# Full experts take silu times up with tokens on partitions and turn only the product; the expert sums move to other banks; the last normalisation runs without GpSimd

## The chip, the cores and the metric

One NeuronCore of a Trainium2 chip. The metric is the device time of one execution, in microseconds (us). TensorE (PE) multiplies and writes PSUM banks of 128 x 512 floats, VectorE (DVE), ScalarE (ACT) and GpSimd (POOL) work on 128 partitions, SyncE (SP) issues transfers. Each engine takes its own instructions in order; semaphores tie the engines together.

## The reference, cut to what matters

Two decoder layers of three mixed branches each; a dense feed-forward follows the first, a mixture of eight experts the second. The change lies in the experts and in the normalisation behind them:

```python
def swiglu(t, w_gu, w_down):
    gate, up = jnp.split(t @ w_gu, 2, axis=-1)
    return (jax.nn.silu(gate) * up) @ w_down

# x: 256 tokens x 1024; eight experts, each w_gu 1024 x 7168 and w_down 3584 x 1024, float32
top_val, top_idx = lax.top_k(logits, 2)
top_w = jax.nn.softmax(top_val, axis=-1)
combine = jnp.sum(jax.nn.one_hot(top_idx, 8) * top_w[..., None], axis=1)
for e in range(8):
    out = out + combine[:, e:e + 1] * swiglu(t, w_gu[e], w_down[e])
h = layer_norm(ALPHA * h + out, ln_ffn_g, ln_ffn_b)
```

## The kernel before, in words

**Precision.** A float32 number is split into a high part (`fp32r`) and the rest, the low part. A product of two float32 matrices is three products: high by high, high by low, low by high.

**Experts and their width.** `route` counts the tokens of each expert. An expert with more than 64 tokens is *full*: its 128 columns of `xe` are tokens, high and low parts being two matrices, and each 2048-column unit of weights takes 12 matmuls of 128 x 512. An expert with up to 64 tokens is a *half* one: `xe` holds the high and low part of each token side by side, so that a gate or up unit goes through PE as raw float32 with 64 columns and needs no split, and a down unit takes 8 matmuls. Which case an expert is in is known on the device only: `tc.If` on a register of each engine chooses. In this input experts 0, 3, 4 and 7 are full, 1, 2, 5 and 6 half (the lines of their matmuls in the trace tell: L1306 is the raw case).

**Steps, slots, units.** An expert has 7 steps (512 inner columns each). A step has six units of 1 MB: two of gate weights (slots 0, 1), two of the down weights of two steps ago (slots 2, 3), two of up weights (slots 4, 5). All steps of all experts form one list of 56, and the loop in `experts` writes out the order of every engine's work by hand (`manual_schedule`). SP loads units into a ring of 11 buffers (`load_unit`, as `make_low` frees them); ACT makes the high part (`make_high`, two units ahead, L1276), DVE the low part (`make_low`, one ahead, L1287); `products` issues the matmuls (L1306, L1311, L1313).

**What the change touches.** Per step `i`, before the change and for both kinds of expert alike:

- `evict(i, 0)` (L1342, slot 2) copies the gate sums from PSUM to `e0`, `evict(i, 1)` (next step's slot 0) the up sums to `e1`. Tokens lie on partitions there.
- `turn(i, half)` (L1348) turns both by four PE transposes each into a `tp` bank: half 0 in slot 4, half 1 in the next step's slot 2.
- `second` (L1352, ACT) and `total` (L1356, DVE) add the two columns of each token of a half expert; for a full expert `total` adds zero times the second, so that it only moves the turned sums back into `e0`, `e1`.
- `silu` (L1360) on the gate, `product` (L1363), then `inner` (L1374 on ACT, L1376 on DVE) writes the high and low part of the product into `f2`, which the down matmuls read.

`combine` (L1418) brings an expert's rows back to token order, two sums per half in `tp` banks, of which there are two; `add` (L1424) adds them to `oa`. `rows` (L1410, L1412) makes the high and low part that `combine` reads. `dispatch(e0)` (L1187 to L1223) gathers the tokens of the next two experts in the odd experts' steps; its last stage makes `sel` on DVE (L1218), turns it on PE (L1219) and copies it on DVE (L1222).

`finish_last` is the end: 8 matmuls (L1574), four `add`s, mean and variance by `bn_stats` on DVE, and one token block's scale and shift on GpSimd and DVE (L1608, L1609), the other's on DVE (L1603, L1605). Behind it every engine loads `cmax` and skips a second pass of the experts (for more than 128 tokens in one) that this input doesn't need.

Of the kernel before, what the change touches and what calls it, by code (L numbers as in the profile page):

```python
# [101 lines left out]
class Builder:  # L102
# [1079 lines left out]
    def dispatch(self, e0):  # L1182
# [27 lines left out]
        ps = self.ptp()  # L1210
        sel = self.tmp("sel", [P, 2, 2 * P], F32R, bufs=1)
        for k in range(2):
            e = slice(e0 + k, e0 + k + 1)

            at = self.tmp("at", [P, P], bufs=1)
            V.scalar_tensor_tensor(at, self.slot2, self.full[:, e], self.slot64, OP.mult, OP.add)
            for t in range(2):
                V.tensor_scalar(sel[:, t, k * P : (k + 1) * P], at, self.pos[:, t, e], None, OP.is_equal)  # L1218
                nc.tensor.matmul(ps[:, k * 256 + t * P : k * 256 + (t + 1) * P], sel[:, t, k * P : (k + 1) * P],  # L1219
                                 self.identr, start=True, stop=True)  # L1220
            st = self.tmp("st", [P, 2, P], F32R, bufs=3)
            V.tensor_copy(st.rearrange("p a b -> p (a b)"), ps[:, k * 256 : k * 256 + 256])  # L1222
            self.slots[e0 + k] = xe[k], st  # L1223
# [67 lines left out]
    def products(self, full, units):  # L1291
# [6 lines left out]
        def some(cases, unsplit):  # L1298
            for k, parts, first, last in units:
# [23 lines left out]
    def experts(self, base, first):  # L1323
# [16 lines left out]
        def evict(i, half):  # L1340
            g[i, half] = self.tmp(f"e{half}", [P, 512], bufs=2 - half)
            ACT(g[i, half], ps.pop((i, half)), AF.Copy)  # L1342

        def turn(i, half):
            tp = ps[i, half, "t"] = self.ptp()
            for q in range(4):
                s = slice(q * P, (q + 1) * P)
                nc.tensor.transpose(tp[:, s], g[i, half][:, s], self.ident)  # L1348

        def second(i, half):  # L1350

            ACT(split4(g[i, half])[:, :, 1, :], split4(ps[i, half, "t"])[:, :, 1, :], AF.Copy)  # L1352

        def total(i, half):
            gv, e = split4(g[i, half]), steps[i][0]
# [3 lines left out]
        def silu(i):  # L1359
            ACT(g[i, 0], g[i, 0], AF.Silu)  # L1360

        def product(i):
            V.tensor_mul(g[i, 1], g[i, 1], g.pop((i, 0)))  # L1363

        def inner(i, part):
# [6 lines left out]
            fv, u = f2[i].rearrange("p q a (n h) -> p a q h n", h=2), split4(g[i, 1])  # L1372
            if part == 0:
                ACT(fv[:, 0], u, AF.Copy)  # L1374
            else:
                V.tensor_sub(fv[:, 1], u, rr(fv[:, 0]))  # L1376
                del g[i, 1]

        def pair(k):
# [17 lines left out]
            self.products(fulls[e], units)  # L1397
# [16 lines left out]
        def combine(e, hf):  # L1414
            for t in range(2):
                sums[e, hf, t] = self.ptp()
# [4 lines left out]
        def add(e, hf):  # L1421
            s = slice(hf * 512, hf * 512 + 512)
            for t in range(2):
                V.scalar_tensor_tensor(self.oa[:, t, s], sums.pop((e, hf, t)), self.comb[:, t, e : e + 1],  # L1424
                                       self.oa[:, t, s], OP.mult, OP.add)

# [4 lines left out]
        with self.tc.manual_schedule():  # L1431
# [8 lines left out]
            for i, (e, j) in enumerate(steps):  # L1440
# [3 lines left out]
                if j == 2:  # L1444
                    value(e + 1)
                if e % 2 and j == 2 and e + 1 < N_EXPERTS:
                    nxt = self.dispatch(e + 1)
                for slot in range(6):
                    idle = slot in (2, 3) and i < 2

                    if slot == 2 and i:
                        turn(i - 1, 1)
                    if slot == 4:
                        turn(i, 0)
# [10 lines left out]
                    if slot == 0 and i:  # L1465
                        evict(i - 1, 1)
                        silu(i - 1)
                    if slot == 2:
                        evict(i, 0)
# [7 lines left out]
                    if slot == 5 and i:  # L1477
                        inner(i - 1, 1)
                    if after is not None and slot in (0, 2):
# [24 lines left out]
                    if slot % 2 == 0:  # L1504
                        pair(k)
# [6 lines left out]
            evict(last, 1)  # L1512
            silu(last)
            turn(last, 1)
            self.make_high(k + 2)
            second(last, 1)
            self.make_low(k + 1)
            total(last, 1)
            pair(k)
# [10 lines left out]
    def moe(self, l):  # L1530
# [13 lines left out]
        rv = nc.values_load(self.cmax[0:1, 0:1], min_val=0, max_val=SEQ)  # L1544
        with self.tc.If(rv > P):
# [6 lines left out]
    def finish_last(self, py, st, comb):  # L1552
# [9 lines left out]
        mv = self.tmp("fl_mv", [P, 2, 2])  # L1562
        rs = self.tmp("fl_rs", [P, 2])
        nm = self.tmp("fl_nm", [P, 1])
        st6 = self.tmp("fl_st", [P, 2, 2, 6], bufs=1)
# [16 lines left out]
        def stats(t, hf):  # L1582
            pin(V.bn_stats(st6[:, t, hf, :], self.oa[:, t, hf * 512 : hf * 512 + 512]))  # L1583

        def aggr(t):
            pin(V.bn_aggr(mv[:, t, :], st6[:, t].rearrange("p a b -> p (a b)")))
            pin(nc.scalar.activation(rs[:, t : t + 1], mv[:, t, 1:2], AF.Sqrt, bias=self.eps))

        x0, y0, x1, y1 = self.oa[:, 0, :], out[:, 0, :], self.oa[:, 1, :], out[:, 1, :]
        add(0, 0)  # L1590
        add(0, 1)
        stats(0, 0)
        stats(0, 1)
        add(1, 0)
        aggr(0)
        pin(V.reciprocal(rs[:, 0:1], rs[:, 0:1]))
        pin(V.scalar_tensor_tensor(nm, mv[:, 0, 0:1], -1.0, rs[:, 0:1], OP.mult, OP.mult))
# [116 lines left out]
```

## Time and profile before

| | us |
|---|---|
| three runs: median (lowest to highest) | 1815.33 (1814.37 to 1815.5) |
| the profiled execution | 1813.66 |
| its span, first to last instruction | 1811.9 |
| around the span | 1.76 |

Durations below are of the profiled execution, so sums are made against its 1813.66 us; the median of the runs lies 1.67 us (0.09%) above. The granted TensorE clock is 0.988 of full speed on the mean, 1.00 in the stretches that matter here. Over the span PE is busy 96%, DVE 72%, ACT 61%, POOL 16%. The experts take from about 890 us to the end.

### The profile page before, as it was taken

What the parts mean: (1) busy time and instruction counts of PE and PEld (TensorE: products, weight loads), DVE (VectorE), ACT (ScalarE), POOL (GpSimd) and SP (SyncE); (2) the same over time, 40 slices, a digit from 0 to 9 for tenths busy, and PEclk for the clock granted to TensorE, in tenths of its full rate; (3) what the DMA queues carried; (4) which work ended last, traced back from release to release, by engine and by line L of the source; (5) the groups of instructions that cost most, each with busy time, mean ns of one, the idle gap of its engine ahead of it and who ended that gap; (6) DMA issues with size and microseconds to landing.
All of it is one profiled execution on the core that took longest, in us unless ns stands there. A gap on an engine that the chain in (4) does not pass through costs nothing. (4 is left out here: it accounts for less than half of the span.)

```text
span 1811.9 us, 28892 instructions
## 1 busy us (share of the span) xinstructions
PE 1737.7 (96%) x10759; PEld 1433.1 (79%) x10759; DVE 1307.0 (72%) x1600; ACT 1097.0 (61%) x1539; POOL 291.0 (16%) x379
## 2 busy tenths in 40 slices
PE   8999999999999999999899999999999999988996
PEld 7989999899998999999788554457888855445784
DVE  7796675865568786665798555579899855557996
ACT  6565564554456665564587455467777745546873
POOL 6115731510033117640000000000000000000000
PEclk8999999999999999999999999999999999999998
DMA  5445545345455545557489999999888999999991
GB/s 211 158 132 185 167 160 173 134 163 184 132 176 173 169 146 194 173 197 273 161 332 361 402 418 418 418 418 418 351 349 345 355 396 419 418 418 419 419 388 47
DMA packets 74848, 497.20 MB, mean 274 GB/s; under 512 B 9340, under 2 KB 10924, under 8 KB 17324
## 3 DMA queue, kind: packets, MB, share of 16 engines
q1 hardware_dynamic: 69200, 486.64, 69.8%
q10 hardware_dynamic: 5468, 8.15, 1.6%
q8 instruction: 114, 1.87, 0.4%
q14 instruction: 66, 0.54, 0.1%
HBM read 493.65 MB, written 1.10 MB: 273 GB/s over the span
## 5 line engine op out<-in xcount | busy, mean ns | idle before, releaser
L1287 DVE TENSOR_TENSOR wlo<-raw,mhi 128x2048 fp32r<-128x2048 f32 x224 | 506.2, 2278 | 102.9 <-ACT mhi L1276 49.0
L1276 ACT ACTIVATE mhi<-raw 128x2048 fp32r<-128x2048 f32 x224 | 424.1, 1904 | 79.3 <-DMA raw<-in_down 47.7
L172 DVE TENSOR_TENSOR w<-raw,w 128x1024 fp32r<-128x1024 f32 (+2 forms) x260 | 320.3, 1232 | 163.4 <-ACT w L171 162.3
L198 PE MATMUL ps_mm<-HL,w 128*128 128x272 f32 (+2 forms) x1344 | 392.5, 292 | 0.8 <-DVE t L393 0.4
L199 PE MATMUL ps_mm<-HL,w 128*128 128x272 f32 (+2 forms) x1344 | 385.3, 287 | 1.1 <-DVE HL L377 1.1
L200 PE MATMUL ps_mm<-HL,w 128*128 128x272 f32 (+2 forms) x1344 | 385.9, 287 | 0.0
L171 ACT ACTIVATE w<-raw 128x1024 fp32r<-128x1024 f32 (+2 forms) x260 | 265.2, 1020 | 119.9 <-PE ps_mm L200 88.9
L198 PEld LDWEIGHTS ps_mm<-HL,w 128*128 128x128 f32 x1344 | 253.3, 188 | 3.9 <-issue 1.4
L199 PEld LDWEIGHTS ps_mm<-HL,w 128*128 128x128 f32 x1344 | 253.1, 188 | 1.7 <-DVE HL L377 1.3
L200 PEld LDWEIGHTS ps_mm<-HL,w 128*128 128x128 f32 x1344 | 253.0, 188 | 0.2 <-DVE w L172 0.2
L1311 PE MATMUL ps_mm<-mhi,xe 128*128 128x512 f32 x888 | 225.3, 395 | 0.1
L1306 PE MATMUL ps_mm<-raw,xf 128*64 128x512 f32 x896 | 201.1, 597 | 0.0
L1311 PEld LDWEIGHTS ps_mm<-mhi,xe 128*128 128x128 f32 x888 | 164.2, 188 | 37.7 <-ACT mhi L1276 1.6
L1311 PE MATMUL ps_acc<-mhi,f 128*128 128x512 f32 x672 | 179.7, 403 | 0.1
L1608 POOL TENSOR_TENSOR raw<-raw,gb 128x768 f32<-128x768 f32 x1 | 1.8, 1801 | 956.1 <-ACT raw L1598 956.1
L1306 PEld LDWEIGHTS ps_mm<-raw,xf 128*64 128x64 f32 x896 | 60.8, 137 | 112.5 <-issue 110.9
L1311 PEld LDWEIGHTS ps_acc<-mhi,f 128*128 128x128 f32 x672 | 124.6, 192 | 23.9 <-issue 0.2
L1313 PE MATMUL ps_acc<-wlo,f 128*128 128x512 f32 x448 | 124.7, 400 | 6.0 <-DVEq L1285 4.6
L1313 PE MATMUL ps_mm<-wlo,xe 128*128 128x512 f32 x444 | 121.3, 394 | 2.2 <-DVE wlo L1287 2.2
L1313 PEld LDWEIGHTS ps_acc<-wlo,f 128*128 128x128 f32 x448 | 85.4, 194 | 29.8 <-DVEq L1285 7.8
L492 POOL TENSOR_SCALAR seg<-b,ctm 128x16 f32<-128x16 f32 (+3 forms) x96 | 101.1, 1071 | 41.7 <-PE ps_acc L534 21.2
L1342 ACT ACTIVATE e<-ps_mm 128x512 f32<-128x512 f32 x112 | 66.8, 596 | 65.3 <-PE ps_mm L1313 50.3
(363 smaller groups left out, 2611.0 us busy)
## 6 DMA issues: line engine op xcount, KB each, us to landing
raw<-in_up SPq DMA_DIRECT2D x224, 1024.0 KB, 11.9
raw<-in_down SPq DMA_DIRECT2D x110, 1024.0 KB, 12.4
raw<-in_g SPq DMA_DIRECT2D x24, 1024.0 KB, 4.9
raw<-in_q SPq DMA_DIRECT2D x12, 1024.0 KB, 5.4
raw<-in_x SPq DMA_DIRECT2D x12, 1024.0 KB, 4.9
raw<-in_dg SPq DMA_DIRECT2D x11, 1024.0 KB, 5.0
raw<-in_du SPq DMA_DIRECT2D x11, 1024.0 KB, 4.8
raw<-in_dd SPq DMA_DIRECT2D x16, 704.0 KB, 4.1
```

What stands on the lines that cost most here:

```text
L171: pin(nc.scalar.activation(hv, src, AF.Copy))
L172: pin((eng or nc.vector).tensor_sub(lv, src, rr(hv)))
L198: nc.tensor.matmul(ps, h, a, start=first and k == 0, stop=False)
L199: nc.tensor.matmul(ps, h, b, start=False, stop=False)
L200: nc.tensor.matmul(ps, lo, a, start=False, stop=last and k == kn - 1)
L492: nc.gpsimd.tensor_scalar(seg[:, j, c0 : c0 + T - l0], ab[:, j, l0:T], self.ctm[:, ki, hd : hd + 1], 0.0, OP.subtract, OP.min)
L1276: d = self.nc.scalar.activation(hi[:, v], self.raws[k][:, v], AF.Copy)
L1287: self.nc.vector.tensor_sub(lo[:, v], self.raws[k][:, v], rr(self.whole[k][:, v]))
L1306: mm(ps[c : c + HALF], rows[:, q % 2 * 4 + i, :], self.raws[k][:, i * 512 : i * 512 + 512], start=bool(first) and i < 2, stop=bool(last) a ...
L1311: mm(ps, a, hv, start=i in first and c == 0, stop=False)
L1313: mm(ps, cases(x)[0], lv, start=False, stop=i in last)
L1342: ACT(g[i, half], ps.pop((i, half)), AF.Copy)
```

## The change

1. **Arms.** `arms` wraps an operation in `tc.If` on one engine with another body for full and half experts. For a full expert: `gate` writes silu of the gate sums straight from PSUM (ACT); `up` is nothing; `times` multiplies the up sums in PSUM by it on DVE (slot 1 of the next step); only half 1 is turned; `inner` reads the turned product from its `tp` bank. `second`, `total`, `product` and the turn of half 0 are skipped. Half experts keep the old order, with `total` a plain add and moved into `product` and `inner`.
2. **Where the turns are issued.** Most turns are issued inside the same If as the matmuls behind them (`before`); in the first two steps of an expert the turn of half 1 has an If of its own.
3. **Banks.** `combine`'s sums and the last stage of `dispatch` come from the four `mm` banks instead of the two `tp` banks. That stage of `dispatch` now makes all of `sel` first, turns it a slot later, and copies it on ACT.
4. **End.** `add` also writes row sums (`accum_out`), the squares are summed on ACT, scale and shift run on DVE alone; the output goes in four transfers of 256 KB, two on SP's queue, two on ACT's. `cmax` is loaded one step before the end.

```diff
@@ dispatch
-        ps = self.ptp()
...
+        if e0:
+            yield
+            yield
+        ps = self.pmm() if e0 else self.ptp()
+        for k in range(2):
+            for t in range(2):
                 nc.tensor.matmul(ps[:, k * 256 + t * P : k * 256 + (t + 1) * P], sel[:, t, k * P : (k + 1) * P],
                                  self.identr, start=True, stop=True)
+        if e0:
+            yield
+        for k in range(2):
             st = self.tmp("st", [P, 2, P], F32R, bufs=3)
-            V.tensor_copy(st.rearrange("p a b -> p (a b)"), ps[:, k * 256 : k * 256 + 256])
+            nc.scalar.activation(st.rearrange("p a b -> p (a b)"), ps[:, k * 256 : k * 256 + 256], AF.Copy)
@@ products.some
+            if before is not None:
+                before(cases is whole)
@@ experts
+        def arms(i, engine, full, half):
+            x = fulls[steps[i][0]]
+            if x is None:
+                if full is not None:
+                    full()
+            elif full is None:
+                with self.tc.If(x[engine] < 1):
+                    half()
+            else:
+                with self.tc.If(x[engine] > 0) as case:
+                    full()
+                if half is not None:
+                    with case.Else():
+                        half()
+        def gate(i):
+            g[i, 0] = self.tmp("e0", [P, 512], bufs=2)
+            x = ps.pop((i, 0))
+            arms(i, on.Activation, lambda: ACT(g[i, 0], x, AF.Silu), lambda: ACT(g[i, 0], x, AF.Copy))
+        def up(i):
+            g[i, 1] = self.tmp("e1", [P, 512], bufs=1)
+            def half():
+                ACT(g[i, 1], ps[i, 1], AF.Copy)
+                ACT(g[i, 0], g[i, 0], AF.Silu)
+            arms(i, on.Activation, None, half)
+        def times(i):
+            arms(i, on.DVE, lambda: V.tensor_mul(g[i, 1], ps[i, 1], g[i, 0]), None)
         def turn(i, half):
             tp = ps[i, half, "t"] = self.ptp()
-            for q in range(4):
+            def go(full):
+                if full and half == 0:
+                    return
+                for q in range(4):
...
         def total(i, half):
-            V.scalar_tensor_tensor(gv[:, :, 0, :], gv[:, :, 1, :], self.half[:, e : e + 1],
-                                   split4(ps.pop((i, half, "t")))[:, :, 0, :], OP.mult, OP.add)
+            V.tensor_add(gv[:, :, 0, :], gv[:, :, 1, :], split4(ps[i, half, "t"])[:, :, 0, :])
         def product(i):
-            V.tensor_mul(g[i, 1], g[i, 1], g.pop((i, 0)))
+            def go():
+                total(i, 1)
+                V.tensor_mul(g[i, 1], g[i, 1], g[i, 0])
+            arms(i, on.DVE, None, go)
@@ inner
+                arms(i, on.Activation, lambda: ACT(fv[:, 0], t, AF.Copy), lambda: ACT(fv[:, 0], u, AF.Copy))
...
+                low = lambda x: V.tensor_sub(fv[:, 1], x, rr(fv[:, 0]))
+                arms(i, on.DVE, lambda: low(t), half)
@@ combine
-                sums[e, hf, t] = self.ptp()
+                sums[e, hf, t] = self.pmm()
@@ the loop over steps and slots
+                    before = None
                     if slot == 2 and i:
-                        turn(i - 1, 1)
+                        before = turn(i - 1, 1)
+                        if j < 2:
+                            with_arms(i - 1, before)
+                            before = None
                     if slot == 4:
-                        turn(i, 0)
+                        before = turn(i, 0)
...
-                    if slot == 3 and i:
-                        total(i - 1, 1)
-                    if slot == 5:
-                        total(i, 0)
+                    if slot == 1 and i:
+                        times(i - 1)
@@ finish_last
-                                       OP.mult, OP.add))
+                                       OP.mult, OP.add, accum_out=part[:, t, hf : hf + 1]))
...
+        for t in range(2):
+            add(t, 0)
+            add(t, 1)
+            m, v = nm[:, t : t + 1], rs[:, t : t + 1]
+            pin(V.tensor_scalar(m, part[:, t, 0:1], part[:, t, 1:2], -1.0 / D_MODEL, OP.add, OP.mult))
+            pin(nc.scalar.activation(junk[t], self.oa[:, t, :], AF.Square, bias=m, accum_out=sq[:, t : t + 1]))
+            pin(nc.scalar.activation(v, sq[:, t : t + 1], AF.Sqrt, scale=1.0 / D_MODEL, bias=self.eps))
+        for t in range(2):
+            x, y, v = self.oa[:, t, :], out[:, t, :], rs[:, t : t + 1]
+            pin(V.scalar_tensor_tensor(y, x, nm[:, t : t + 1], g, OP.add, OP.mult))
+            pin(V.reciprocal(v, v))
+            for hf in range(2):
+                s = slice(hf * 512, hf * 512 + 512)
+                pin(V.scalar_tensor_tensor(y[:, s], y[:, s], v, b[:, s], OP.mult, OP.add))
+                eng = nc.scalar if hf else nc.sync
+                pin(eng.dma_start(self.out[0, t * P : (t + 1) * P, s], y[:, s]))
```

## Rows read from the trace of the kernel before

**Rows 1.** Stretches: us; busy PE, weight loads, DVE, ACT, POOL; clock; DMA share; GB/s.

```profile
1118.00:1196.00 78.00, 68.31 (x300) 35.16 (x299) 40.11 (x39) 34.91 (x42) 0.00 (x0) 0.96 1.01 419
1262.00:1457.00 195.00, 193.51 (x898) 158.35 (x897) 171.67 (x123) 149.51 (x141) 0.00 (x0) 1.00 0.90 354
1704.00:1774.70 70.70, 70.70 (x326) 57.72 (x325) 64.85 (x41) 55.81 (x49) 0.00 (x0) 1.00 0.90 365
```

**Rows 2.** The chain that ended last, in expert 7: start, us, what.

```profile
1704.49 1.85 PE ps_mm L1311 x8
...
1707.25 1.86 PE ps_mm L1311 x8
...
1715.61 0.44 PE ps_tp L1348 x4
...
1722.04 1.15 PE ps_mm L1311 x5
```

**Rows 3.** PE's waits, 1195 to 1460: us in total, times, longest.

```profile
PE ps_tp L1348 <- DVE oa L1424: 2.0, 2, 1.6
PE ps_tp L1418 <- DVE e L1356: 1.7, 1, 1.7
PE ps_mm L1313 <- DVE wlo L1287: 1.1, 1, 1.1
PE ps_tp L1219 <- DVE sel L1218: 1.1, 1, 1.1
```

**Rows 4.** Timeline of PE in expert 7: start, us, instruction [idle before <- releaser].

```profile
1690.29 0.73 PE L1418 MATMUL ps_tp<-sel,st 128*128 128x512 f32 x2 [1.68 <-DVE e L1356]
...
1697.84 0.65 PE L1348 MATMUL ps_tp<-ident,e 128*128 128x128 f32 x4 [0.39 <-DVE oa L1424]
```

**Rows 5.** Groups of DVE, 1704 to 1774: shapes, count | busy us, mean ns.

```profile
L1287 DVE TENSOR_TENSOR wlo<-raw,mhi 128x2048 fp32r<-128x2048 f32 x25 | 56.7, 2289 | 3.5 <-ACT mhi L1276 1.5 <-PE ps_acc L1311 0.9 <-PE ps_mm L1313 0.8
L1356 DVE SCALAR_TENSOR_TENSOR e<-e,rt_all,ps_tp 128x256 f32<-128x256 f32 x8 | 3.8, 479 | 1.3 <-ACT e L1352 1.3
L1376 DVE TENSOR_TENSOR f<-e,f 128x512 fp32r<-128x512 f32 x4 | 2.8, 692 | 1.0 <-ACT f L1374 1.0
L1363 DVE TENSOR_TENSOR e<-e,e 128x512 f32<-128x512 f32 x4 | 2.8, 692 | 0.1
```

**Rows 6.** Timeline of ACT in a half expert.

```profile
1190.72 1.90 ACT L1276 ACTIVATE mhi<-raw 128x2048 fp32r<-128x2048 f32 x1
1192.74 0.60 ACT L1342 ACTIVATE e<-ps_mm 128x512 f32<-128x512 f32 x1
```

**Rows 7.** Timeline, expert 4's third step: start, us, instruction.

```profile
1367.38 1.09 PE L1418 MATMUL ps_tp<-sel,st 128*128 128x512 f32 x4
1368.05 1.41 DVE L1424 SCALAR_TENSOR_TENSOR oa<-ps_tp,rt_all,oa 128x512 f32<-128x512 f32 x2 [1.34 <-PE ps_tp L1418]
...
1372.17 2.28 DVE L1287 TENSOR_TENSOR wlo<-raw,mhi 128x2048 fp32r<-128x2048 f32 x1
...
1373.83 1.08 PE L1418 MATMUL ps_tp<-sel,st 128*128 128x512 f32 x4
```

**Rows 8.** Timeline of the end.

```profile
1793.13 3.70 PE L1574 MATMUL ps_mm<-ys,st 128*128 128x512 f32 x8 [0.45 <-ACT ys L1568]
...
1794.30 1.61 DVE L1579 SCALAR_TENSOR_TENSOR oa<-ps_mm,rt_all,oa 128x512 f32<-128x512 f32 x2 [3.64 <-PE ps_mm L1574]
...
1802.92 2.63 DVE L1605 SCALAR_TENSOR_TENSOR raw<-raw,fl_rs,gb 128x1024 f32<-128x1024 f32 x1
...
1806.38 0.33 SPq L1610 DMA_DIRECT2D out<-raw  x1
```

**Rows 9.** Groups of ACT over the mixer: the accumulator's read.

```profile
L614 ACT ACTIVATION_READ_ACCUMULATOR b<-b,att_nm 128x1 f32 x32 | 6.0, 187 | 0.0
```

**Rows 10.** Groups of DVE, 868 to 885: a two-tensor operation of 1024 with GpSimd idle.

```profile
L992 DVE SCALAR_TENSOR_TENSOR oa<-oa,lt_mv,seg 128x1024 f32<-128x1024 f32 x2 | 2.5, 1254 | 0.0
```

More of the change, by code (lines that the diff above doesn't have):

```diff
@@ L1289, in make_low, with products @@
         self.load_unit()
-    def products(self, full, units):
+    def products(self, full, units, before=None):
         mm = self.nc.tensor.matmul
@@ L1350, in second @@
         def second(i, half):
-            ACT(split4(g[i, half])[:, :, 1, :], split4(ps[i, half, "t"])[:, :, 1, :], AF.Copy)
+            def go():
+                ACT(split4(g[i, half])[:, :, 1, :], split4(ps[i, half, "t"])[:, :, 1, :], AF.Copy)
+            arms(i, on.Activation, None, go)
         def total(i, half):
-            gv, e = split4(g[i, half]), steps[i][0]
-            V.scalar_tensor_tensor(gv[:, :, 0, :], gv[:, :, 1, :], self.half[:, e : e + 1],
-                                   split4(ps.pop((i, half, "t")))[:, :, 0, :], OP.mult, OP.add)
@@ L1371, in inner, with half, pair @@
                     f2[i] = self.tmp("f2", [P, 4, 2, P], F32R, bufs=1)
-            fv, u = f2[i].rearrange("p q a (n h) -> p a q h n", h=2), split4(g[i, 1])
+            fv = f2[i].rearrange("p q a (n h) -> p a q h n", h=2)
+            t, u = split4(ps[i, 1, "t"]), split4(g[i, 1])
             if part == 0:
-                ACT(fv[:, 0], u, AF.Copy)
+                arms(i, on.Activation, lambda: ACT(fv[:, 0], t, AF.Copy), lambda: ACT(fv[:, 0], u, AF.Copy))
             else:
-                V.tensor_sub(fv[:, 1], u, rr(fv[:, 0]))
-                del g[i, 1]
-        def pair(k):
+                low = lambda x: V.tensor_sub(fv[:, 1], x, rr(fv[:, 0]))
+                nxt = i + 1 if i + 1 < len(steps) else None
+                same = nxt is not None and steps[nxt][0] == steps[i][0]
+                def half():
+                    low(u)
+                    if same:
+                        total(nxt, 0)
+                arms(i, on.DVE, lambda: low(t), half)
+                if nxt is not None and not same:
+                    arms(nxt, on.DVE, None, lambda: total(nxt, 0))
+        def pair(k, before=None):
             kind, i, _ = self.units[k]
@@ L1396, in pair @@
                                   (0, 1) if j == 0 and q == 0 else (), (2, 3) if j == NJ - 1 and q else ()))
-            self.products(fulls[e], units)
+            self.products(fulls[e], units, before)
         def unsplit(e):
@@ L1445, in experts @@
                     value(e + 1)
+                if base == 0 and i == len(steps) - 2:
+                    self.most = nc.values_load(self.cmax[0:1, 0:1], min_val=0, max_val=SEQ)
                 if e % 2 and j == 2 and e + 1 < N_EXPERTS:
@@ L1478, in experts @@
                         inner(i - 1, 1)
+                    if slot == 5 and i == 0:
+                        arms(0, on.DVE, None, lambda: total(0, 0))
                     if after is not None and slot in (0, 2):
@@ L1504, in experts @@
                     if slot % 2 == 0:
-                        pair(k)
+                        pair(k, before)
                     if slot == 5 and done is not None:
@@ L1511, in experts @@
             last = len(steps) - 1
-            evict(last, 1)
-            silu(last)
-            turn(last, 1)
+            up(last)
+            times(last)
+            before = turn(last, 1)
             self.make_high(k + 2)
+            self.make_low(k + 1)
+            pair(k, before)
             second(last, 1)
-            self.make_low(k + 1)
-            total(last, 1)
-            pair(k)
             product(last)
@@ L1590, in finish_last @@
[L1590 to L1597, printed above, removed]
-        pin(nc.scalar.activation(y0, x0, AF.Identity, scale=rs[:, 0:1], bias=nm))
-        add(1, 1)
-        stats(1, 0)
-        stats(1, 1)
-        aggr(1)
-        pin(V.scalar_tensor_tensor(y1, x1, mv[:, 1, 0:1], g, OP.subtract, OP.mult))
```

43 lines of the change are left out of this document (15 added, 28 removed).

## The prediction

> **What bounds the kernel now.** I read first the stretches of the experts [rows 1]. In a full expert PE is busy without a gap (70.70 of 70.70 us, 193.51 of 195.00) at full clock while the transfers stand at 0.90 of the DMA engines: PE sets the pace, and the ring of weights fills up ahead of it. In a half expert it is the other way round: 1.01 of the DMA engines, 419 GB/s, PE 68.31 of 78.00. A step's six units of 1.049 MB take 6.29 / 0.419 = 15.0 us to load, whatever the engines do. So work saved in a half expert is worth nothing, and work that PE is spared in a full one shows at once, also behind a half one: at the end of a full expert the ring is full, SP loads a unit when PE frees one, and the stream that bounds the next half expert starts earlier by what the full one saved.
>
> Next the chain in a full expert, to see what a step is made of [rows 2]. It is PE alone: 1704.49 to 1722.04, 17.55 us a step, of which each of the two turns takes 0.44 us (1715.61, and the same again before 1722.04); the rest, 16.67, is six units of 2.76 to 2.78. A full step then needs 17.55 us on PE and 15.0 of transfers, 2.5 us apart.
>
> Third, where PE does wait in full experts. From 1195 to 1460 [rows 3] it waits 1.7 us for DVE's `total` before the second sum of `combine` (the two `tp` banks are taken by a turn and the first sum), 1.6 + 0.4 for `add` before a turn (the same banks), 1.1 in `dispatch` for `sel`, and 1.1 + smaller ones at the entry of expert 3, where the raw units land just in time. Around expert 7 [rows 4] it is 1.7 and 0.4. `combine` runs in the second and third step of an expert, so three of its seven runs lie in full experts (3, 4 and 7), four in half ones.
>
> **The change, part by part.**
>
> *The turn left out.* 28 full steps (4 x 7) lose one turn of 0.44 us on PE: 12.3 us. DVE must keep below the new step of 17.1 us. Before it has 6 x 2.29 + 2 x 0.48 + 2 x 0.69 = 16.1 us a step [rows 5]; the two `total`s go, `times` takes the place of `product`, and the low part reads PSUM instead of SBUF (nearest row: the same operation at 0.69), so 15.1. ACT loses a copy of 0.6 and two `second`s. The transfers need 15.0. So PE stays the bound, by 2 us. The new wait is the turn of half 1 on `times`: `times` stands on DVE behind the low parts of slots 0 and 1, the turn on PE behind 5.55 us (two units) of matmuls of slot 0. The up sums are complete as slot 0 begins; the low part of slot 1 can run then, because its buffer is freed at that moment, 2.3 us, then `times`, 0.7: 3.0 against 5.55, so 2.5 us to spare. Behind the turn wait only PE's own matmuls. Four of the 28 turns lie in the first two steps of experts 3 and 7, where the units land just in time; I count half of those: 24 x 0.44 + 4 x 0.22 = **11.4 us**. Bounds: 12.3, and 0 if PE pays for the skip itself (a rival below).
>
> *The arms.* What a skipped arm costs shows on ACT, which already skips `make_high` in half experts [rows 6]: the instruction before ends at 1192.62, the next starts at 1192.74, 0.12 us, where neighbours otherwise overlap by 0.05; so 0.17. A full step gets three such skips on ACT and one or two on DVE, 0.5 and 0.3 us, hidden by ACT's 55.81 and DVE's 64.85 of 70.70 us [rows 1] and the work that goes. A half step gets two to four on each, hidden by the transfers: PE has 15.0 x (1 - 68.31/78) = 1.9 us a step to spare there, ACT and DVE half their time. If that cover were gone it would be up to 0.7 us x 28 half steps. PE's own branches before (two a pair) leave no gap in [rows 2]. Taken: 0.
>
> *The banks of `combine`.* The waits of 1.7 + 1.6 + 0.4 [rows 3] and 1.7 + 0.4 [rows 4], 5.8 us in all, are on `tp` banks that `combine` no longer uses. What is late next: of the four `mm` banks in turn, the second `combine`'s first sum takes the one that holds the last step's up sums, and these are now freed by `times` on DVE (before, by ACT's copy in slot 0). On DVE stand ahead of `times`: two `add`s, a low part, the low part of `rows`, another low part. In expert 4 [rows 7] that queue ran from the first `combine` at 1367.38 to the end of its second low part at 1374.45; `times` 0.69 more is 1375.14, 7.8 us behind the start, while PE stands at the second `combine` at 1373.83, 6.45 behind: a wait of 1.3 us. Three times that is 3.9; with 0.3 more each where DVE starts late (experts 3 and 7) 4.5. Gain 5.8 - 4.5 = **1.3 us**; bounds 5.8 (no wait) and -1 (DVE as late as it is now at 3 and 7).
>
> *`dispatch`.* The 1.1 us wait for `sel` goes, since DVE now makes it two slots ahead of PE; the one in expert 3 counts, those of 1 and 5 lie under transfers: **1.1 us**. The first `dispatch`, ahead of expert 0, also changes, in an order that the planner chooses: 0, bounds -1 and 1.
>
> *The end.* DVE's first `add` starts at 1794.30, PE's last sum is complete at 1793.13 + 3.70 = 1796.83 [rows 8]. Four `add`s of 0.7 [rows 7], four reads of an accumulator and two means, taken as 0.2, bring DVE to 1798.3. The read I take at 0.19, ACT's row [rows 9]; bounds 0 and 0.19 each. [...] Then DVE's chain: scale by g, 1.25 us without GpSimd beside it [rows 10] against 2.63 with it [rows 8], a reciprocal taken as 0.2, two halves of 0.7, for each block: 2 x 2.85 = 5.7, minus 0.1 of overlap. Squares and roots run on ACT meanwhile. The last transfer is issued at 1803.9 instead of 1806.38: 2.5. From there to the span's end at 1811.9 it is 5.5 us today, with nothing busy: a transfer and the engines' way out. I take 0.2 off for the register load that moves and the queues that leave side by side: **2.7 us**; bounds 1.5 and 4.
>
> Sum: 11.4 + 1.3 + 1.1 + 2.7 = 16.5 us. The profiled execution would be 1813.66 - 16.5 = 1797.2; the runs' median lies 1.67 above it: 1815.33 - 16.5 = **1798.8 us**.
>
> **Rivals.**
>
> *PE pays for the skip.* If the skipped turn makes PE wait for its own last matmul, as ACT does in [rows 6], most of 0.44 a step is lost. For: [rows 6]. Against: a turn is skipped inside an arm that has matmuls, and pairs whose arms differ (12 against 8 matmuls a unit) leave no gap today. A third to nothing of 11.4 would be left: gain 5 to 9, time 1806 to 1810.
>
> *The banks come free in time.* DVE has 1 us less a step, so `times` may run ahead of the second `combine`: 4.5 us more, and up to 1 of the end: 1793 to 1795. Against: the `add`s that start the queue wait for PE, not for DVE's own work (the 1.34 in [rows 7]).
>
> *Nothing gained:* the full experts' gain is taken back by transfers. The stream is idle for 10% of the full stretches and would have to speed up by 2.6%; against it, then, [rows 1]. With the end alone: 1812 to 1816.
>
> *Slower: a jump out of the loaded code.* The two arms of a pair grow, and every engine jumps more often. What a far jump costs at most is seen at the end, 5.2 us from 1806.71 to 1811.9, in which each engine skips the second pass. Once per expert would be 8 x 5.2, of which the four in half experts are hidden: 21 us lost, 1820 us. It decides from the fourth jump on PE's path on. Against: today's four Ifs a full step on ACT, four on DVE and three on PE leave no gap in [rows 2]. [...]
>
> **How the numbers follow.** Forecast, with its own range 1794 to 1804: 0.62. PE pays (1804 to 1811): 0.16. Banks in time, or more (below 1794): 0.07. Nothing gained, within 0.2% or 3.6 us, which is about what a measurement can tell: 0.08. Slower: 0.07. Faster is 0.62 + 0.16 + 0.07 = 0.85. The range leaves out the last two (0.15) and half of the fast end (0.03): 1791.5 to 1811.
>
> **What would show it.** After: a full step of 17.1 us in the chain, one turn of 0.44 in it; 112 transposes in full experts instead of 28 x 8 = 224; DVE without a wait of PE on `times` outside the third steps; there a wait of PE at `combine` of 1 to 1.5 us named for DVE's product; the half experts at 419 GB/s as before, starting earlier; the last output transfer issued 10.8 us behind the first of the final matmuls instead of 1806.38 - 1793.13 = 13.25. The prediction is wrong if gaps appear on PE at the skipped turn, if a turn waits for `times` in every step, if the half experts are no longer bound by transfers, or if the last issue is not earlier.

## The result, and the profile after

| | before | after |
|---|---|---|
| median of four runs each (lowest to highest), us | 1814.85 (1814.3 to 1815.5) | 1906.35 (1906.15 to 1907.7) |
| ratio, 95% interval | | 1.0505, 1.0489 to 1.0522 |
| span of the profiled execution, us | 1811.9 | 1904.8 |

Slower by 5%, 91.5 us, where 16.5 us less was forecast. The busy time of the engines over the span, from the page of the profile after (us, share, instructions), names the engine: ACT's work rises from 61% to 73% of a longer span, while the diff takes instructions from it.

```profile
PE 1756.8 (92%) x10647; PEld 1426.0 (75%) x10647; DVE 1270.7 (67%) x1537; ACT 1382.5 (73%) x1686; POOL 288.5 (15%) x377
```

ACT's groups over the whole span of the kernel after, shapes kept apart (count | busy us, mean ns | idle before), say with what:

```profile
L1284 ACT ACTIVATE mhi<-raw 128x2048 fp32r<-128x2048 f32 x222 | 421.7, 1911 | 11.0 <-ACTq L1357 4.2 <-PE ps_mm L1321 2.6 <-PE ps_mm L1316 1.8
...
L1284 ACT ACT_TABLE_LOAD x104 | 133.4, 1283 | 14.5 <-ACTq L1357 11.7 <-PE ps_acc L1323 0.9 <-PE ps_mm L1199 0.3
L1429 ACT ACT_TABLE_LOAD x41 | 52.6, 1283 | 36.5 <-DVEq L1293 18.3 <-PE ps_acc L1323 14.3 <-PE ps_tp L1396 2.6
L1372 ACT ACT_TABLE_LOAD x28 | 35.9, 1283 | 0.5
L1380 ACT ACT_TABLE_LOAD x28 | 35.9, 1283 | 0.5
L1403 ACT ACT_TABLE_LOAD x28 | 35.9, 1283 | 11.8 <-ACTq L1282 5.8 <-PE ps_tp L1396 4.8 <-DVE oa L1489 1.1
```

The five groups of loads alone are 229 loads of ACT's function table, 1.283 us each, 293.7 us. No row of the prediction has such a load, and the diff shows none: they stand in the built program, whose order is shown under the first experiment. (In the kernel after L1372 is `gate`, both its arms; L1284 `make_high`, L1403 `second`, L1379 and L1380 the half arm of `up`, L1429 and L1431 `inner`, L1386 `times`, L1396 the turn, L1483 `combine`, L1489 `add`, L1293 and L1295 `make_low`. L1282 is the If around `make_high`, L1357 and L1360 are those of `arms`; a row that names such a line with an engine's queue, as ACTq or DVEq, means that engine's passing of the If.)

Windows of the kernel after, columns as in [rows 1]: a stretch of half experts 1 and 2, and three full steps at the end of expert 4.

```profile
1100.00:1180.00 80.00, 70.53 (x316) 34.84 (x315) 42.23 (x44) 65.92 (x71) 0.00 (x0) 0.98 1.01 416
1461.50:1521.00 59.50, 52.65 (x231) 41.08 (x229) 45.15 (x26) 56.05 (x40) 0.00 (x0) 1.00 0.82 318
```

In the full stretch ACT is busy 94% and sets the pace; PE, which had no gap in [rows 1], is at 88%, the transfers at 0.82 instead of 0.90. In the half experts the transfers still run at 416 GB/s, but ACT's share has gone from 45% to 82%. One of the three full steps on ACT (timeline, us):

```profile
1465.80 1.28 ACT L1284 ACT_TABLE_LOAD   x1 [0.23 <-ACTq L1357]
1467.10 3.71 ACT L1284 ACTIVATE mhi<-raw 128x2048 fp32r<-128x2048 f32 x2
1470.83 1.28 ACT L1372 ACT_TABLE_LOAD   x1
1472.12 0.60 ACT L1372 ACTIVATE e<-ps_mm 128x512 f32<-128x512 f32 x1
1472.74 1.28 ACT L1284 ACT_TABLE_LOAD   x1
1474.04 1.92 ACT L1284 ACTIVATE mhi<-raw 128x2048 fp32r<-128x2048 f32 x1
1476.26 1.28 ACT L1284 ACT_TABLE_LOAD   x1 [0.30 <-ACTq L1357]
1477.55 1.92 ACT L1284 ACTIVATE mhi<-raw 128x2048 fp32r<-128x2048 f32 x1
1479.48 1.28 ACT L1429 ACT_TABLE_LOAD   x1
```

Five loads a step, each directly ahead of an instruction; `gate`'s silu (L1372) is the only one of these instructions that is not a copy. Turn to turn (PE's timeline) the step is 1489.54 - 1469.79 = 19.75 us:

```profile
1469.79 0.63 PE L1396 MATMUL ps_tp<-ident,e 128*128 128x128 f32 x4 [1.12 <-DVE e L1386]
1489.54 0.63 PE L1396 MATMUL ps_tp<-ident,e 128*128 128x128 f32 x4 [1.14 <-DVE e L1386]
```

It was 17.55 [rows 2]. At both turns PE waits for `times`. The silu was ready long before (1472.12 + 0.60). But `times` ends a row of work on DVE without a gap, and that row starts only when ACT hands over the high part of `inner` (1480.78 + 0.63), for which DVE stood 3.22 us (DVE's timeline):

```profile
1481.50 0.69 DVE L1431 TENSOR_TENSOR f<-ps_tp,f 128x512 fp32r<-128x512 f32 x1 [3.22 <-ACT f L1429]
1482.10 6.68 DVE L1295 TENSOR_TENSOR wlo<-raw,mhi 128x2048 fp32r<-128x2048 f32 x3
1488.71 0.68 DVE L1386 TENSOR_TENSOR e<-ps_mm,e 128x512 f32<-128x512 f32 x1
```

The number of turns is as intended: 336 transposes, 8 in each of 28 half steps, so 112 in the full ones.

### The profile page after: what moved, and what is told of

Read it like the earlier page. It is cut to its first block, busy times and chain, and to the rows that moved or that the text cites. A ratio compares the mean times of both kernels' runs of the same rounds, so it can differ in the third digit from the quotient of the medians.

```text
span 1904.8 us, 30033 instructions
## 1 busy us (share of the span) xinstructions
PE 1756.8 (92%) x10647; PEld 1426.0 (75%) x10647; DVE 1270.7 (67%) x1537; ACT 1382.5 (73%) x1686; POOL 288.5 (15%) x377
## 5 line engine op out<-in xcount | busy, mean ns | idle before, releaser
L1295 DVE TENSOR_TENSOR wlo<-raw,mhi 128x2048 fp32r<-128x2048 f32 x224 | 503.9, 2277 | 157.5 <-ACTq L1282 70.3
L1284 ACT ACTIVATE mhi<-raw 128x2048 fp32r<-128x2048 f32 x224 | 423.7, 1903 | 11.0 <-ACTq L1357 4.2
L1321 PE MATMUL ps_mm<-mhi,xe 128*128 128x512 f32 x888 | 230.0, 402 | 1.8 <-ACT mhi L1284 1.6
L1321 PEld LDWEIGHTS ps_mm<-mhi,xe 128*128 128x128 f32 x888 | 170.7, 193 | 43.6 <-ACT mhi L1284 2.5
L1321 PE MATMUL ps_acc<-mhi,f 128*128 128x512 f32 x672 | 184.8, 411 | 8.4 <-ACTq L1282 8.4
L1323 PEld LDWEIGHTS ps_mm<-wlo,xe 128*128 128x128 f32 x444 | 81.6, 189 | 64.3 <-DVE wlo L1295 47.9
```

The lines of the kernel that those rows point to most:

```text
L1284: d = self.nc.scalar.activation(hi[:, v], self.raws[k][:, v], AF.Copy)
L1295: self.nc.vector.tensor_sub(lo[:, v], self.raws[k][:, v], rr(self.whole[k][:, v]))
L1321: mm(ps, a, hv, start=i in first and c == 0, stop=False)
L1323: mm(ps, cases(x)[0], lv, start=False, stop=i in last)
```

## Experiments

Each kernel ran beside the kernel before, whose medians were 1815.07 us (beside one load, the end, the banks and the turn), 1814.78 (the loads put back in full and in half experts, the product, the first `dispatch`), 1814.86 (one statement earlier, the four loads), 1814.23 (without arms, and the best) and 1814.79 (`total`).

**One load ahead of the experts.** The order of ACT's instructions in the built program shows where the loads come from. The routing's exponential (L1168) leaves its own table (loaded just ahead of it, 1.283 us at L1168, in the run below where silu's was there before); then come `gate`'s two arms, and the next high part behind them (semaphore instructions left out):

```
L1168 ACTIVATE rt_all<-rt_all 128x2
L1360 COMPARE_AND_BRANCH
L1372 ACT_TABLE_LOAD
L1372 ACTIVATE e<-ps_mm 128x512
L1360 UNCONDITIONAL_BRANCH
L1372 ACTIVATE e<-ps_mm 128x512
L1360 UNCONDITIONAL_BRANCH
L1282 COMPARE_AND_BRANCH
L1284 ACT_TABLE_LOAD
L1284 ACTIVATE mhi<-raw 128x2048
```

The first L1372 is the full arm's silu, the second the half arm's copy. The full arm leaves silu's table; the half arm has no load, so it leaves the exponential's. Behind these arms even a copy has a load, and silu's table is loaded again at every silu of all 56 steps: 28 loads at L1372, in the full steps, and 28 at L1380, in the half ones. My reading is that a load stands where the arms ahead of it leave different tables. Then none is left if silu's table is there before the first arm, so that both arms leave it.

```diff
         if base == 0:
             self.route_end()
+            self.table("silu_and_others")
```

> The changed kernel with one line added: the activation table with Silu is loaded once, ahead of the experts, so that both sides of every branch on ACT leave the same table and none has to be loaded again behind a branch. Theory (reloads): about 250 loads of 1.283 us go; ACT drops from 19.15 of 20 us in a full stretch to about 15; PE sets the pace again with full steps of 17.1 us; the time is that of the prediction's sum, 1799 us, with its range 1792 to 1811. Rival 1 (the branches themselves, their jumps and skips on ACT and DVE, are the cost and the loads only fill time in which ACT waited anyway): above 1860 us. Rival 2 (PE's wait of 1.1 us at the turn for DVE's product is not a consequence of the late ACT): the waits stay at 24 of 28 turns and the time is about 1799 + 27 = 1826 us.

Measured: 1804.09 us, ratio 0.9941 (0.9925 to 0.9958). No load is left in the experts but this one. Windows of a half and a full stretch (columns as above), and two turns of PE's timeline:

```profile
1100.00:1180.00 80.00, 70.16 (x312) 35.59 (x308) 39.75 (x37) 38.32 (x46) 0.00 (x0) 0.96 1.01 418
1400.00:1451.00 51.00, 51.00 (x229) 41.69 (x228) 42.67 (x25) 34.53 (x23) 0.00 (x0) 1.00 0.95 371
```
```profile
1407.40 0.60 PE L1396 MATMUL ps_tp<-ident,e 128*128 128x128 f32 x4
1424.38 0.60 PE L1396 MATMUL ps_tp<-ident,e 128*128 128x128 f32 x4
```

PE is busy without a gap again, a step takes 16.98 us, the waits at the turns are gone. The 102 us between the two kernels go with the loads; rivals 1 and 2 fall. It lies 5 us above the forecast, which the other runs take up.

**The same line one statement earlier**, ahead of `route_end`.

> The changed kernel with the same one line as the first of these kernels (load the table with Silu once), but one statement earlier, ahead of the routing's exponential, which takes another table. Theory: what counts is the table that both sides of the first branch find, so this line changes nothing: about 250 loads in the experts and 1906 us. Rival (the load itself, or its wait, was what the changed kernel lacked): 1804 us.

Measured: 1908.99 us; the five groups of loads have the same counts as in the kernel after, and the exponential (L1168) has a load of its own. So it is the table that the first two arms find that counts.

**Loads put back in full experts only**, one in each of ACT's five arms:

```diff
+            if engine == on.Activation and x is not None:
+                go = full
+                def full():
+                    nc.scalar.preload_act_table_set("silu_and_others")
+                    if go is not None:
+                        go()
```

> The first kernel (one table load ahead of the experts) with five table loads put back into each step of the full experts alone, one in each of ACT's five arms (140 loads of 1.283 us). Theory: ACT's step is six high parts of 1.91, two copies of 0.6, 6.4 of loads and about 0.85 around branches, 20.0 us against the 17.05 that TensorE needs, so 28 x 2.9 = 82 us more than the first kernel: about 1886 us. Rival (the loads fill time in which ACT waits anyway): under 10 us more.

Measured: 1847.85 us, 43.8 more than without, half of the 82 expected. Turn to turn it is 18.94 us:

```profile
1436.56 0.63 PE L1404 MATMUL ps_tp<-ident,e 128*128 128x128 f32 x4 [1.10 <-DVE e L1394]
1455.50 0.63 PE L1404 MATMUL ps_tp<-ident,e 128*128 128x128 f32 x4 [1.13 <-DVE e L1394]
```

That is ACT's work and nothing else: six high parts of 1.91, two copies of 0.6, five loads of 1.283, 19.1 with their overlaps uncounted. The 0.85 that I had added for branches is not there: in this kernel no arm of a full expert is skipped. In the kernel after three are. (28 x 1.96 would be 54.9. Some steps hide the loads: by the starts of TensorE's steps the first ones of experts 3 and 7 take 17.3 to 17.4 us with and without them, and the fourth one of expert 4 takes 17.1.)

**Four loads in the two arms that run** in a full step, the other three arms skipped empty:

```diff
+            def full():
+                load()
+                ACT(g[i, 0], x, AF.Silu)
+                load()
```

and around the copy of `inner` one load ahead and two behind. The two that stand together show as one in the trace, which has 112 loads, four a step.

> The first kernel with four table loads in each full step, all of them in the two arms that run there (gate and inner), so that the other three arms are skipped with nothing in them, as in the changed kernel. With ACT as the bound a step is 12.65 us of work and 5.13 of loads, and what the three skips cost. Theory (a skip takes 0.2 to 0.3 us of ACT that shows once ACT sets the pace): steady steps of 18.6 us, about 36 us more than the first kernel, 1840 us. Rival (skips are free, ACT only pays its work): steady steps of 17.8 us, about 17 us more, 1821 us.

Measured: 1846.64 us, 42.6 more than without. Turn to turn 18.65 us:

```profile
1436.47 0.63 PE L1402 MATMUL ps_tp<-ident,e 128*128 128x128 f32 x4 [0.95 <-DVE e L1392]
1455.12 0.63 PE L1402 MATMUL ps_tp<-ident,e 128*128 128x128 f32 x4 [1.48 <-DVE e L1392]
```

Between, ACT stands still ahead of three high parts (its timeline), as it does ahead of loads in the kernel after, where it waits for its own branches (0.23 and 0.30 in the step shown):

```profile
1450.05 1.92 ACT L1284 ACTIVATE mhi<-raw 128x2048 fp32r<-128x2048 f32 x1 [0.20 <-PE ps_mm L1321]
1452.22 3.72 ACT L1284 ACTIVATE mhi<-raw 128x2048 fp32r<-128x2048 f32 x2 [0.25 <-DVE wlo L1295]
...
1461.40 1.92 ACT L1284 ACTIVATE mhi<-raw 128x2048 fp32r<-128x2048 f32 x1 [0.32 <-PE ps_acc L1323]
```

0.20 + 0.25 + 0.32 = 0.77 us, close to 18.65 - 12.65 - 5.13 = 0.87: so much do three skips cost once ACT sets the pace. With no arm skipped, the step of 18.94 above is 0.13 below the same sum with five loads. One more load makes 18.65 + 1.28 = 19.93, the kernel after has 19.75. A full step after is its work, five loads and three skips.

**Loads put back in half experts only**, in the same way.

> The first kernel (one table load ahead of the experts) with five table loads in each step of the half experts alone, one in each of ACT's five arms (140 loads of 1.283 us). Theory: ACT has 35 of 78 us of work there, 6.7 us a step, so 13.1 with the loads, below the 15.0 of the transfers; hidden but for the steps in which the ring is still full, so 0 to 26 us more than the first kernel. Rival (a load costs the same wherever it stands): as much as in the full experts, 60 us or more.

Measured: 1828.01 us, 23.9 more: of 140 x 1.283 = 179.6 us most is hidden, not all. Around the start of expert 2 the transfers keep their pace, 413 GB/s, but ACT is at 73.08 of 80 us. Experts 1 and 5, several of whose steps took 12 to 14 us on a full ring, can't run ahead any more: each takes 105.7 us where it took 95.1.

```profile
1100.00:1180.00 80.00, 68.99 (x310) 35.60 (x306) 42.84 (x39) 73.08 (x74) 0.00 (x0) 0.98 1.01 413
```

The same split stands in the traces of the kernel after and of the one with one load, by the start of TensorE's first matmul of an expert (us):

```
              after   one load    later by
expert 1     1021.8     1006.4        15.4
expert 3     1234.2     1206.1        28.1
expert 5     1521.0     1453.0        68.0
expert 7     1730.5     1652.8        77.7
span's end   1904.8     1802.2       102.6
```

In full experts (0, 3 and 4, 7) 15.4 + 39.9 + 24.9 = 80.2 us, 2.9 a step; in half ones 12.7 + 9.7 = 22.4.

**The end alone**, on the kernel before.

> The kernel before with nothing but the new end (no GpSimd, no bn_stats, four output transfers on two queues). Prediction's term: 2.7 us faster, bounds 1.5 and 4, so 1812.6 us (ratio 0.9985). Rival (the end is bounded by what comes behind the last issue): ratio 1.000.

Measured: 1810.71 us, ratio 0.9974 (0.9965 to 0.9984): 4.4 us (2.9 to 6.4 by the interval), above the bound of 4, but not clearly. The timeline of the end of the kernel after:

```profile
1889.97 3.70 PE L1645 MATMUL ps_mm<-ys,st 128*128 128x512 f32 x8 [0.45 <-ACT ys L1639]
...
1891.81 0.08 DVE L1651 DVE_READ_ACCUMULATOR oa<-ps_mm,rt_all,oa 128x1 f32 x1
...
1900.18 0.35 ACTq L1671 DMA_DIRECT2D out<-raw  x1
```

The last issue is 10.21 us behind the first final matmul (10.8 expected, 13.25 before [rows 8]), a read of the accumulator takes 0.08 (0.19 taken), and from the issue to the end it is 4.6 (5.5 before).

**The banks of `combine` undone**, on the kernel with one load: `self.pmm()` back to `self.ptp()` in `combine`.

> The first of these kernels (one table load ahead of the experts) with the sums of combine put back into the two banks of the turns; dispatch stays as changed. By the prediction's term the new banks gain 1.3 us, so this one takes 1.3 us more than the first. If the mm banks come free in time it is 4.5 to 5.8 us more; if nothing of combine lies on PE's path, 0.

Measured: 1807.31 us, 3.2 more than with the new banks. The wait of 1.3 us for DVE's product that I had put against them does not appear: with one load, PE's only wait from 1330 to 1451, with two `combine`s in it, is this one (engine, line waited for: us, times, longest):

```profile
PE ps_tp L1396 <- DVE e L1386: 0.3, 1, 0.3
```

In experts 3 and 7 (1195 to 1262, 1640 to 1710) no wait at `combine` appears either. With the old banks the turns wait for `add` again, in 1195 to 1262, 1640 to 1710 and 1330 to 1451 in turn, 3.5 us in all, close to the 3.2:

```profile
PE ps_tp L1396 <- DVE oa L1489: 1.7, 1, 1.7
PE ps_tp L1396 <- DVE oa L1489: 0.9, 1, 0.9
PE ps_tp L1396 <- DVE oa L1489: 0.9, 1, 0.9
```

**The turn put back** in full experts (`if full and half == 0: return` taken out; its bank is read by nobody).

> The first of these kernels with the turn that a full expert leaves out put back on TensorE (four transposes of the gate half into a bank that nobody reads). By the prediction's term it takes 11.4 us more than the first (28 times 0.44 less half of four), bounds 12.3 and 0. If the full steps are bound by DVE, ACT or the transfers in the first kernel, it takes less than 3 us more.

Measured: 1816.58 us, 12.5 more than without it. TensorE does not pay for the skip. The traces of the two (their profiled executions, 1818.84 and 1803.92 us, lie 14.9 apart) also tell whether a gain of a full expert comes through the half ones behind it (first matmul of a step, us):

```
                          one load   turn put back   later by
expert 1                    1006.4          1010.7        4.3
expert 3, fourth step       1260.2          1265.6        5.4
expert 5                    1453.0          1463.6       10.6
expert 7, fourth step       1705.8          1718.8       13.0
```

It does: what TensorE is behind as experts 1 and 5 start it is still behind in the fourth steps of experts 3 and 7.

**The product ahead of the low part.** With one load, in half experts, PE waits at the turn of the up half (PE's waits in 1100 to 1212, then one case in the timeline):

```profile
PE ps_tp L1396 <- DVEq L1360: 14.2, 6, 4.1
```
```profile
1191.94 1.91 ACT L1284 ACTIVATE mhi<-raw 128x2048 fp32r<-128x2048 f32 x1 [5.71 <-DMA raw<-in_down]
1193.76 0.58 ACT L1379 ACTIVATE e<-ps_mm 128x512 f32<-128x512 f32 x1
1193.89 2.29 DVE L1295 TENSOR_TENSOR wlo<-raw,mhi 128x2048 fp32r<-128x2048 f32 x1 [7.19 <-ACT mhi L1284]
...
1196.38 1.09 PE L1396 MATMUL ps_tp<-ident,e 128*128 128x128 f32 x4 [4.10 <-DVEq L1360]
```

What it turns is ready when ACT's copy ends at 1194.34. But the turn also waits until DVE has passed the place of `times`, which a half expert skips, and that place stands behind a low part that waits for a landing.

```diff
+                    if slot == 1 and i:
+                        times(i - 1)
                     if not idle:
                         self.make_low(k + 1)
...
-                    if slot == 1 and i:
-                        times(i - 1)
```

> The first kernel (one table load ahead of the experts) with the product of gate and up moved on VectorE from behind the low part of slot 1 to ahead of it. In half experts that product is skipped, but TensorE's turn of the up half still waits until VectorE has passed its place, and that place stands behind a low part which waits for a landing: in expert 2 of the first kernel 14.2 us in 6 waits, the longest 4.1. Theory: these waits shrink to about 1.7 each as in the kernel before, TensorE enters experts 3 and 7 about 3 us less behind the landing, and the time falls by 2 to 4 us, to about 1801 us. Rival 1: the transfers set the pace of half experts whatever TensorE waits for, no change, 1804 us. Rival 2: in full experts VectorE now waits for the up sums ahead of a low part that is due, up to 0.5 us in each of 28 steps, slower by up to 14 us.

Measured: 1801.49 us, ratio 0.9926 (0.9909 to 0.9942). The wait for DVE's place is gone; the turn now waits for ACT's copy, 6.7 us in 4 (3.5 in 3 in the kernel before). The 2.6 us are as expected, but no wider than the intervals of the two, and the traces do not show where they come from: from 1100 to 1212 TensorE waits 15.0 us in all where it waited 15.4, because others take the place, 2.9 us for the first low part of expert 3 among them, and the profiled executions are only 0.9 apart (1803.06, 1803.92). So the wait for a skipped place is shown, its price is not.

**The first dispatch's copies back on VectorE**, besides. With one load, at the entry of the experts (timeline, three engines):

```profile
899.69 0.66 ACT L1230 ACTIVATE st<-ps_tp 128x256 fp32r<-128x256 f32 x2 [5.01 <-PE ps_tp L1224]
...
900.47 0.17 DVE L1169 TENSOR_SCALAR rt_all<-rt_all 128x2 f32<-128x2 f32 x1 [5.03 <-ACT rt_all L1168]
...
903.72 1.19 PE L1323 MATMUL ps_mm<-wlo,xe 128*128 128x512 f32 x4 [2.16 <-DVE wlo L1295]
```

The copies stand ahead of the exponential on ACT, and a low part behind it on DVE.

> The kernel with the product ahead of the low part, and the first dispatch's copies back on VectorE. In the first kernel ACT stands 5.0 us at these copies, with the exponential of the routing behind them, VectorE 5.0 us for that, and TensorE 2.2 us for a low part behind it. Theory: 2 to 3 us less than the kernel with the product ahead alone, about 1798 us. Rival: the entry is bounded by the first units' landing, no change.

Measured: 1799.18 us, ratio 0.9914 (0.9898 to 0.9931), 2.3 less than the one before it.

**Without arms, and the best once more.**

> The change without its arms: the kernel before with the new end, the mm banks for combine, the later dispatch (the first one's copies on VectorE) and the earlier register load; every expert still copies, turns both halves and multiplies with tokens in the free dimension. From the single runs: end 4.4, banks 3.2, dispatch 1.1 by the prediction, 8.7 us less than the kernel before, 1806 us. Rival (the banks only help where the product frees them early): the end alone, 1810 us.

> The best kernel so far (one table load ahead of the experts, the product ahead of the low part, the first dispatch's copies on VectorE), in more rounds beside the kernel without arms. If the arms are worth what putting the turn back cost (12.5 us) less what the half experts lose, it is 5 to 10 us faster than the kernel without arms: 1799 us, ratio 0.9914 as before. Rival (all of the gain is the end, the banks and dispatch): no difference between the two.

Measured: without arms 1803.29 us, ratio 0.9935 (0.9921 to 0.9948); the best 1799.74, 0.9915 (0.9902 to 0.9929). So end, banks, `dispatch` and the register load that moves bring 10.9 us, all arms together 3.5 more. The two intervals still overlap, though each of the five runs of the best lies below each of the five without arms. The traces show when TensorE starts a step (first matmul of its first unit, us):

```
start of              without arms    best    difference
expert 1                    1006.7  1004.4          -2.3
expert 3                    1202.9  1202.3          -0.6
expert 3, fourth step       1257.2  1257.3          +0.1
expert 5                    1454.9  1449.9          -5.0
expert 7                    1652.4  1648.0          -4.4
expert 7, fourth step       1704.5  1701.8          -2.7
expert 7, last step         1757.1  1753.1          -4.0
```

In full steps from the fourth on the arms gain 0.4 to 0.5 us each; between the start of expert 1 and the fourth step of expert 3 they lose 2.4 us of it again, and 2.3 from expert 5 to the fourth step of expert 7. These are the two stretches, without arms and in the best (columns as in [rows 1]):

```profile
1006.70:1257.20 250.50, 235.12 (x1094) 136.66 (x1094) 160.37 (x148) 149.02 (x176) 0.00 (x0) 1.00 1.01 418
1454.90:1704.50 249.60, 234.37 (x1085) 137.55 (x1085) 159.12 (x144) 147.49 (x174) 0.00 (x0) 0.99 1.01 417
```
```profile
1004.40:1257.30 252.90, 235.16 (x1081) 136.91 (x1081) 156.20 (x143) 143.27 (x164) 0.00 (x0) 0.99 1.01 417
1449.90:1701.80 251.90, 235.65 (x1073) 138.33 (x1073) 155.30 (x139) 142.87 (x163) 0.00 (x0) 0.98 1.01 417
```

It is not the transfers that take the gain back. They run at the same rate in both kernels, and in the best they have 2.4 and 2.3 us more until TensorE gets to the fourth step, some 1 MB or one unit. So they keep their lead; what is lost lies between the landing of a unit and its matmul. TensorE is idle for 17.7 instead of 15.4 us in the first stretch; in the second for 16.3 instead of 15.2, and busy 1.3 us longer. Its granted clock is 0.99 and 0.98 instead of 1.00 and 0.99 on the mean; whether that is part of the loss or comes of the waiting was not tested. In the best kernel PE waits for the first low part of expert 3 (its timeline):

```profile
1207.39 1.19 PE L1326 MATMUL ps_mm<-wlo,xe 128*128 128x512 f32 x4 [2.98 <-DVE wlo L1298]
```

**`total` behind the low part**, in an arm of its own.

> The best kernel with one more undoing: VectorE's sum of the gate half (total) stands behind the low part of slot 5 again, in an arm of its own, instead of ahead of it. In the best kernel, on the way from the half experts 2 and 6 into the full ones, that sum waits 1.5 us for ACT's copy, the first low part of the full expert stands behind it, and TensorE waits 2.98 us for that low part at 1207 and 2.68 at 1653 (0.8 in the kernel without arms). Theory: both waits fall to about 0.8, 4 us less, about 1796 us (ratio 0.9895). Rival 1: the next unit's landing is what ends the wait then, no change, 1799.7. Rival 2: one more skipped arm on VectorE in each full step, where it is busy 0.90 of the time, costs 0.3 us a step, 8 us more.

Measured: 1798.61 us, ratio 0.9903 (0.9886 to 0.992). The wait fell as said:

```profile
1206.00 1.20 PE L1326 MATMUL ps_mm<-wlo,xe 128*128 128x512 f32 x4 [1.04 <-DVE wlo L1298]
```

The time fell by 1.1 us, not by 4, and not measurably; the fourth step of expert 7 starts at 1701.8 as before. So this wait alone is not what takes the gain back. Which operation does stays open.

## Why the prediction was wrong

*The arms* is the step that failed: "Taken: 0", with "ACT loses a copy of 0.6 and two `second`s". I took ACT's instructions from the diff. The built program has five more in each full step, and with silu's table loaded ahead of the first arms (1804.09 us) none of them is left. They cost 102 us; the cover I named, ACT at 55.81 of 70.70 us [rows 1], holds 14.9 us over four steps, 3.7 a step, against 6.4 of loads. The half steps were not all "hidden by the transfers" either: loads put back there cost 23.9 us. No rival had this; the one that ends slower (a jump out of the loaded code) had the sign, not the mechanism, and nothing here bears it out. The 0.17 for a skip on ACT was nearly right (0.20 to 0.32 of standing still; the overlap of neighbours, 0.05 in it, is 0.10 beside the skip in the trace of before, 1189.72 + 0.58 against 1190.20), and hidden only while ACT does not set the pace.

With the loads gone the forecast of 1798.8 stands against 1804.09, which lies in the stated range partly by luck: the arms bring far less than their term, the end, the banks and `dispatch` more than theirs. Term by term:

- *The turn left out*, 11.4: putting it back costs 12.5, and the step is 16.98 against 17.1. "Work that PE is spared in a full one shows at once, also behind a half one" held for it (4.3 and 10.6 us at the start of experts 1 and 5, 5.4 and 13.0 behind the half ones). But the arms as a whole bring 3.5 in the best kernel, and by estimate 1 as the change orders them (3.5 - 2.6), so something else in them costs 9 to 11.5 us: "Taken: 0" fails a second time, without loads. Some 7 of it stand in the table above: of 2.3 and 5.0 us in hand at the start of experts 1 and 5, nothing and 2.7 are left at the fourth steps of experts 3 and 7, where three more turns of 0.44 should have been gained each time. "2.5 us to spare" for the turn's wait on `times` held in full experts but for waits of up to 0.9 in experts 3 and 7; what the same wait does where `times` is skipped I had left out.
- *The banks*, 1.3 with bounds -1 and 5.8: 3.2. The queue on DVE that I worked out from [rows 7] does not delay `times` enough; in that the rival in which the banks come free in time, given 0.07, was right, but not in its size: 5.8 in all. Without arms the banks, `dispatch` and the register load together bring (0.9974 - 0.9935) x 1814 = 7.1 us, beyond the 1.3 and 1.1 of the terms.
- *`dispatch`*: the first one, taken as 0 with bounds -1 and 1, costs 2.3, by a copy queued on ACT ahead of the exponential. The 1.1 for the later ones was not tested alone.
- *The end*, 2.7: 4.4; the reads of the accumulator are half as long (0.08 against 0.19) and the way out 0.9 shorter.
- *PE pays for the skip*: no. *Nothing gained*, the gain taken back by transfers: much of it is taken back, but the transfers keep their lead.

## What to carry to other kernels

Count an engine's instructions in the built program, not in the diff: where a branch on ACT has silu in one arm and a copy in the other, look for table loads behind it (229 of 1.283 us here), and load the table ahead of the first branch, behind the last use of another (1804.09 us; ahead of that use 1908.99). When an operation becomes conditional, ask what waits for its place on its engine in the case that skips it (4.10 us in one case here), and what stands ahead of that place. One part of a change can lose what another saves, so price it by a run without the whole change too, not only by undoing the part that saves.

## What the runs showed of the hardware

A table load takes 1.283 us on the mean, in the 140 of the kernel with loads in full experts, which load the table that is already there, as in the 229 of the kernel after. The instruction behind it starts at once (1470.83 + 1.28, next at 1472.12), and a load behind silu or a copy does too (1472.12 + 0.60, next at 1472.74), but where a skipped arm lies between (0.23 and 0.30). In the kernel after the loads stand behind branches that leave different tables; in the kernel with one load ahead of the experts no instruction of theirs has one. That TensorE's turn waits for a skipped instruction's place on another engine, up to 4.10 us, I had not expected either.
